# A hybrid decoder block on one core: the output projection in two seven-product parts with tokens on the result's partitions, and last products whose banks begin with a partial sum

## Chip, core and metric

One core of a Trainium2 chip runs the whole program in one launch. The metric is the device time in microseconds (us) of one execution; the number to be predicted is the median of several runs. Engines are named as in the profile: PE (TensorE), DVE (VectorE), ACT (ScalarE), POOL (GpSimd) and SP (SyncE, which here only issues transfers). PEld is PE's loading of the stationary operand.

## The reference

One layer of a decoder, 512 tokens of width 2048, all in fp32. The part that matters here begins with `mix`, the sum of two gated mixers:

```python
mix = (g_a * y_a + g_b * y_b) @ w_o[l]          # (512 x 2048) @ (2048 x 2048)
x = x + gt_a * mix                              # called x2 below
h = _rmsnorm(x, norm_ffn[l]) * (1.0 + sc_f) + sh_f
gate, up = jnp.split(h @ w_gate_up[l], 2, axis=-1)   # 2048 x 11264
x = x + gt_f * ((jax.nn.silu(gate) * up) @ w_down[l])  # 5632 x 2048
return _rmsnorm(x, final_norm)
```

`gt_a`, `sc_f`, `sh_f` and `gt_f` are one value for each of the 2048 channels.

## The kernel before

**Precision.** Every large product is computed from operands split in two: a high half rounded to fp32r (`hi`, made by ACT) and the rest (`lo`, made by DVE). A product is three matmuls, hi·hi, hi·lo and lo·hi, added up in a PSUM bank. Raw weights come from HBM through SP's queue into five `raws` buffers; four `his` and four `los` buffers hold the halves; 68 `slots` of 128 x 512 hold nearly everything else. There are eight PSUM banks of 128 x 512.

**Order.** The work is a list of `Unit`s (load, split, matmuls, `pre`, `post`), which a `Driver` runs with loads and splits some units ahead. Side work stands in generators that are stepped between matmuls. Every operation is recorded (so all have the line number 482 in the profile) and a planner, `Score`, then puts out the instructions: those of PE, POOL and SP stay in the order of the program, those of DVE and ACT are placed by due times from a model of costs.

**The output projection.** Up to this point the activations have channels on the partitions. `yb_done` makes, from four row blocks of `mix` at a time, the operands of a seven-product scheme of matrix multiplication (2 x 2 blocks, seven products instead of eight): a11, a12, a21, a22 and the combinations x5, x6, x7, x3. It also stores a21 in HBM. `strassen_wo(n)` for n = 0, 1, 2 then computes 512 output channels each: eight units, one for each pair of row blocks of 128; in each, the seven products times two halves of 128 channels times three matmuls. The weights are the stationary operand and 256 tokens are the moving one, so results have channels on the partitions. The last 512 channels come from `half_sets`, a plain product for each half of the tokens (h = 0, 1), for which `wo_rest` brings a21 back.

**x2 and its norm.** The results are multiplied by `gt_mix` and added to x (from the transposed input `xT`): for n = 0, 1 by accumulating transfers of POOL's queue into `x2_dram`, which had been filled with a copy of x, and for n = 2 and the plain set in SBUF. `squares` adds up squares over channel tiles; `part_rstd` sums them over partitions with matmuls by a column of ones (`hss`), takes the root on DVE, and `spread` brings it to all partitions with another matmul (`hbc`). For h = 0 this runs under the plain set's second half, for h = 1 under the first gate-up set. `h2_gen(h)` then makes for each pair of channel tiles the scaled and shifted `h2f` and its two halves, `h2T`.

**Gate-up.** `gu0` (h = 0, then h = 1) and `gu_both(1)` are plain products with 256-column matmuls: unit i of 16 reads h2T tile i of its half. From then on `big` uses the seven-product scheme in two parts: `FIRST4` (m1, m6, m7, m5: eight units of 24 matmuls of 512 columns) and `LAST3` (m2, m4, m3: eight units of 18), with tokens on the result's partitions and weight combinations that the first part stores in `s_dram` for the second. `tokens_down` does the same for the down projection.

**The last products.** `last_dn` ends the kernel. Its first 16 units are the last `tokens_down`; meanwhile partial sums come back (`s_t`, from `down_dram`), are multiplied by the row of `gt_f` (`gated`), and x2 is loaded back. Then four row blocks of w_down remain for each token tile t and 512 columns n. `last_weights` multiplies those weights by the row of `gt_f` and splits them. Each `token_unit` begins its bank with four transposes of x2 (`turned`), since x2 has channels on the partitions, and adds the products; `finished` adds s_t to the bank, squares it (with the sum along the row on ACT), multiplies by `final_norm`, and after the last columns of a token tile takes the root and stores. The last tile's columns are done in two halves of 256.

Of the kernel before, what the change touches and what calls it, by code (L numbers as in the profile page):

```python
# [9 lines left out]
F32 = mybir.dt.float32  # L10
# [481 lines left out]
def block_kernel(ctx: ExitStack, tc: tile.TileContext, a: dict, out):  # L492
# [1102 lines left out]
    a21 = [None] * 4  # L1595
    a21_dram = dram.tile([4, P, 512], F32, name="a21_dram")

    def yb_done(n):
        def done(ps):
# [6 lines left out]
            def gen():  # L1606
                a1 = S("a1h", F32R), S("a1l", F32R)
                for i in (2 * n, 2 * n + 1):
# [7 lines left out]
                    side(a21_dram[n, :, c], a21_)  # L1616
                    u, v = S("x56"), S("x73")
                    x5, x6, x7, x3 = (w[:, 256 * h:256 * h + 256] for w in (u, v) for h in range(2))
                    for o, x, y, op in ((x5, a22, a21_, ALU.subtract), (x6, a11, x5, ALU.add), (x7, a11, a21_, ALU.subtract),
                                        (x3, x6, a12, ALU.subtract)):  # L1620
                        nc.vector.tensor_tensor(o, x, y, op)
# [27 lines left out]
    def wo_half(k, h, xi):  # L1649

        n, j = divmod(k, 4)
        i = 2 * n + j % 2
        if j > 1:
            return wo_part("m4" if h else "m2", i, xi)
        return a21[n][xi][:, 256 * (i % 2):256 * (i % 2) + 256] if h else wo_part("m1", i, xi)

    def strassen_wo(n):

        w = a["w_o"][0].rearrange("(n h k p) c -> n k p h c", n=4, h=2, p=P)

        def outputs(res):
            for h in range(2):
                for f in range(2):
                    t, q, gate = res.pop("gp"[f] + str(h)), 2 * n + f, (gt_mneg if f else gt_mix)
                    if n == 2:
                        for k in (2 * q, 2 * q + 1):
                            d = half_of(x2[h][q], k)
                            nc.vector.scalar_tensor_tensor(d, half_of(t, k), gate[:, k:k + 1], d, op0=ALU.mult, op1=ALU.add)
                        squares(q, HALF[h], nc.vector)
                        nc.scalar.dma_start(x2_dram[h, q], x2[h][q][:])  # L1670
                    else:
                        for k in (2 * q, 2 * q + 1):
                            nc.scalar.activation(half_of(t, k), half_of(t, k), AF.Copy, scale=gate[:, k:k + 1])
                        side(x2_dram[h, q], t[:], accum_op=ALU.add)
                    del t
                    yield

        def freed(i):
            if n == 2:
                wo_x["x56"][i] = wo_x["x73"][i] = None  # L1680
                if i == 5:
                    for q in (4, 5):
                        for h in range(2):
                            load_x2(h, q)

        return strassen(lambda i: w[i // 2, i % 2], 512 * n + 256, 512 * n,
                        [(c, i, j, lambda k, c=c: [wo_part(c, k, xi) for xi in range(2)]) for c, i, j in PRODUCTS],
                        wo_ready, outputs, freed)

    def wo_rest():  # L1690

        def x2_back(h):
            for q in range(4):
                x2[h][q] = S("x2")
                side(x2[h][q][:], x2_dram[h, q])

        for h in range(2):
            x2_back(h)
        for n in range(4):
            a21[n] = S("a21")  # L1700
            load(a21[n][:], a21_dram[n])
            yield
        for q in range(4):
            squares(q, HALF[0], nc.vector)
            if q % 2:
                yield
        for n in range(4):
            a21[n] = hilo(a21[n][:], "a21")
            yield
        for q in range(4):  # L1710
            squares(q, HALF[1], nc.vector)
            yield

# [17 lines left out]
    x2 = [[None] * 8 for _ in range(2)]  # L1731
    s_ffn, sh_ffn, gt_mix, gt_ffn, gt_mneg = (C(n, [P, 16]) for n in ("s_ffn", "sh_ffn", "gt_mix", "gt_ffn", "gt_mneg"))
    g_dram = dram.tile([D], F32, name="g_dram")
    x2_dram = dram.tile([2, 8, P, 512], F32, name="x2_dram")
# [6 lines left out]
    def x_part(h, q):  # L1741
        return a["xT"][256 * q:256 * q + 256, 256 * h:256 * h + 256].rearrange("(k p) n -> p k n", p=P)

    def load_x2(h, q):
        x2[h][q] = S("x2")
        load(x2[h][q][:].rearrange("p (k n) -> p k n", k=2), x_part(h, q))

    def copy_x(h, q):
        side(x2_dram[h, q].rearrange("p (k n) -> p k n", k=2), x_part(h, q))

    sums = {}

    def add_gated(h, k, ps, gate, c0=0):

        d = half_of(x2[h][k // 2], k)[:, c0:c0 + ps.shape[1]]
        nc.vector.scalar_tensor_tensor(d, ps, gate[:, k:k + 1], d, op0=ALU.mult, op1=ALU.add)

    def view(tile_, seg):

        return tile_[:].rearrange("p (k n) -> p k n", k=2)[:, :, seg[1]:seg[1] + seg[2]]  # L1760

    def squares(q, seg, eng):

        s = S("sq")
        st = sums.setdefault(seg, [])
        nc.scalar.activation(view(s, seg), view(x2[seg[0]][q], seg), AF.Square)
        if st and eng is not None:
            eng.tensor_tensor(view(st[0], seg), view(st[0], seg), view(s, seg), ALU.add)
        else:
            st.append(s)  # L1770
# [1282 lines left out]
```

## Time and profile before

| | |
|---|---|
| median of 3 runs | 2698.59 us (2698.04 to 2701.13) |
| the profiled execution, its own time | 2699.31 us |
| its span, first to last instruction | 2697.5 us |
| mean granted clock of PE | 0.999 |
| PE busy | 2683.8 us of the span (99%) |
| DVE busy | 2124.2 us (79%) |
| ACT busy | 1168.9 us (43%) |
| transfers | 587.16 MB, mean 218 GB/s |

A matmul's row has a start and a duration that includes its drain, so matmuls that follow each other closely overlap in the rows: 512 columns show 0.39 us each while they start 0.2267 us apart. Paces are therefore taken from stretches of many matmuls, or from starts. A row of the chain of waits reads: start, length, engine and tile, and the number of instructions merged in it. Names of tiles have their final numbers cut off: `x2` appears as `x`, `h2f` stays, `rs` are the small tiles of a root, `dnt` the banks of the last products.

### The profile page before, as it was taken

The numbers are of one execution on the slowest core, as the hardware profiler recorded it, in microseconds if no ns is written. First come the engines' busy times: TensorE is split into PE (matmuls) and PEld (weight loads), VectorE is DVE, ScalarE is ACT, GpSimd is POOL, SyncE is SP. The second block draws the span as 40 slices with busy tenths as digits, with TensorE's granted clock in tenths as the row PEclk, the third lists the DMA queues.
The fourth block names the chain that finished last, engine by engine and source line by source line (L and its number), as shares of the span: only waits on it lengthen the run. The fifth ranks groups of instructions, "written<-read, shape, count | busy, mean of one in ns | idle before, by whom it ended". The sixth has DMA issues, their size and how long they took to land.

```text
span 2697.5 us, 38122 instructions
## 1 busy us (share of the span) xinstructions
PE 2683.8 (99%) x13886; PEld 2277.0 (84%) x13886; DVE 2124.2 (79%) x3259; ACT 1168.9 (43%) x1620; POOL 196.7 (7%) x315
## 2 busy tenths in 40 slices
PE   9999999999999999999999999999999999999998
PEld 7888788888888888889999888888888888888887
DVE  8985656777887887688897777887777888878888
ACT  4343432452245343234574444444444445444434
POOL 0000002001101000000100000000000101010000
PEclk9999999999999999999999999999999999999999
DMA  9995555646566889624864565656556667695694
GB/s 351 348 369 193 165 168 170 199 132 189 166 195 208 302 280 333 235 83 124 258 194 144 189 204 201 211 198 209 188 201 206 212 231 270 198 278 205 222 311 164
DMA packets 308228, 587.16 MB, mean 218 GB/s; under 512 B 42228, under 2 KB 81412, under 8 KB 308040
## 3 DMA queue, kind: packets, MB, share of 16 engines
q1 hardware_dynamic: 267832, 493.60, 55.2%
q0 software_dynamic: 20992, 64.27, 7.3%
q10 hardware_dynamic: 19216, 26.87, 2.8%
q8 instruction: 108, 1.77, 0.3%
q14 instruction: 80, 0.66, 0.1%
HBM read 501.77 MB, written 83.89 MB: 217 GB/s over the span
## 4 chain that ended last, share of the span: by engine, by line
PE 98%; DMA 1%; DVE 0%; ACT 0%; issue 0%; DVEq 0%; SPq 0%
PE m L482 45%; PE gb L482 7%; PE v L482 4%; PE gu L482 3%; PE z L482 3%; PE ya L482 3%; PE ga L482 3%; PE k L482 3%; PE q L482 3%; PE yb L482 3%; PE s L482 3%; PE dnt L482 2%; PE wo L482 2%; PE qk L482 2%; PE cq L482 2%; PE dn L482 2%
## 5 line engine op out<-in xcount | busy, mean ns | idle before, releaser
L482 ACT CAST hi<-raws 128x1024 fp32r<-128x1024 f32 (+2 forms) x360 | 325.8, 905 | 509.7 <-PE m L482 298.8
L482 DVE TENSOR_TENSOR lo<-raws,hi 128x1024 fp32r<-128x1024 f32 (+2 forms) x360 | 369.1, 1039 | 171.1 <-ACT hi L482 167.5
L482 ACT CAST hi<-raw 128x1024 fp32r<-128x1024 f32 (+2 forms) x259 | 268.8, 1038 | 483.0 <-DMA raw<-in_w_in_dram 80.3
L482 DVE TENSOR_TENSOR lo<-raw,hi 128x1024 fp32r<-128x1024 f32 (+2 forms) x259 | 313.3, 1211 | 170.7 <-ACT hi L482 163.0
L482 DVE CUSTOM_DVE_ANT_0 rawm<-rawm,cbc 128x1024 f32<-128x1024 f32 x192 | 232.4, 1224 | 21.7 <-DMA rawm<-in_w_mod_dram 21.4
L482 ACT CAST hi<-sums 128x1024 fp32r<-128x1024 f32 x136 | 143.0, 1051 | 160.3 <-PE m L482 133.7
L482 DVE TENSOR_TENSOR lo<-sums,hi 128x1024 fp32r<-128x1024 f32 x136 | 166.2, 1222 | 47.5 <-ACT hi L482 47.2
L482 PE MATMUL m<-hi,h2h 128*128 128x512 f32 x480 | 189.9, 396 | 0.0
L482 PE MATMUL m<-hi,h2l 128*128 128x512 f32 x480 | 187.2, 390 | 0.0
L482 PE MATMUL m<-lo,h2h 128*128 128x512 f32 x480 | 187.1, 390 | 0.0
L482 PE MATMUL m<-lo,xh 128*128 128x512 f32 x448 | 174.5, 390 | 0.8 <-DVE lo L482 0.8
L482 PE MATMUL m<-hi,xh 128*128 128x512 f32 x448 | 174.4, 389 | 0.0
L482 PE MATMUL m<-hi,xl 128*128 128x512 f32 x448 | 174.3, 389 | 0.0
L482 DVE TENSOR_TENSOR sums<-raws,raws 128x1024 f32<-128x1024 f32 x112 | 136.6, 1219 | 8.8 <-DMA raws<-in_w_down_dram 4.5
L482 POOL DMA_DIRECT2D s_dram<-raws x112 | 60.9, 543 | 679.2 <-DVE raws L482 657.2
L482 PEld LDWEIGHTS m<-hi,h2l 128*128 128x128 f32 x480 | 90.1, 188 | 18.8
L482 PEld LDWEIGHTS m<-lo,h2h 128*128 128x128 f32 x480 | 90.3, 188 | 17.8
L482 PEld LDWEIGHTS m<-hi,h2h 128*128 128x128 f32 x480 | 90.2, 188 | 17.6
L482 PE MATMUL gb<-hh,hi 128*128 128x512 f32 x256 | 101.9, 398 | 0.0
L482 PEld LDWEIGHTS m<-lo,xh 128*128 128x128 f32 x448 | 84.1, 188 | 19.0 <-DVE lo L482 1.7
L482 PE MATMUL gb<-hl,hi 128*128 128x512 f32 x256 | 100.0, 390 | 0.0
L482 PE MATMUL gb<-hh,lo 128*128 128x512 f32 x256 | 99.9, 390 | 0.0
(543 smaller groups left out, 7089.8 us busy)
## 6 DMA issues: line engine op xcount, KB each, us to landing
raws<-in_w_gate_up_dram SPq DMA_DIRECT2D x400, 256.0 KB, 3.6
rawm<-in_w_mod_dram SPq DMA_DIRECT2D x192, 512.0 KB, 5.5
raw<-in_w_in_dram SPq DMA_DIRECT2D x143, 512.0 KB, 4.8
raws<-in_w_down_dram SPq DMA_DIRECT2D x160, 256.0 KB, 4.6
s_dram<-raws POOLq DMA_DIRECT2D x112, 256.0 KB, 3.2
raws<-s_dram SPq DMA_DIRECT2D x112, 256.0 KB, 2.9
rawa<-in_w_in_dram SPq DMA_DIRECT2D x32, 512.0 KB, 3.7
raws<-in_w_o_dram SPq DMA_DIRECT2D x48, 256.0 KB, 3.0
```

The source lines that it names most:

```text
L482: self.tc.keep_in_program_order(op.call(*op.args, **op.kwargs))
```

## The change

Four things change.

1. `tokens_wo(n)` for n = 0, 1 takes the place of the three channel-wise sets and the plain one. It has the form of `big`: activations are the stationary operand, 512 weight columns the moving one, 1024 output channels a part, all with tokens on the result's partitions. The signs of x5, x6 and x3 change for it; a21 is no longer stored. In the second part (n = 1) the product m4 is taken out of the last eight units and done at the very end (`fourth`, eight units of six matmuls), so that tokens 0 to 255 are complete before it starts.
2. x2 is kept by tokens: x comes from an untransposed input, the gate is a row spread over the partitions (`mix_row`), the squares are summed along the row by ACT, and `rooted` takes a root per token on DVE and scales x2 with it. No matmuls by ones remain.
3. `h2_gen` now transposes the scaled x2 on PE, four 128 x 128 tiles to a bank (`hT`), and scales and shifts them out of PSUM: on ACT for h = 0, on DVE for h = 1. It is stepped only by `ahead`, in front of each unit of `gu0`.
4. In the last products no transposes are left. `seeded` writes the bank before its first matmul: for n = 1, 3 DVE writes s_t + x2, for n = 0, 2 (`RAW`) ACT writes s_t. In the RAW columns neither the weights nor s_t are multiplied by the row of `gt_f`; `finished` multiplies the bank instead and adds x2. In the other columns `finished` reads the bank directly for the square and for the product with `final_norm`.

The core of the diff:

```diff
-    def strassen_wo(n):
...
-    def wo_rest():
...
+    def tokens_wo(n):
+        c0, c1 = 1024 * n, 1024 * n + 512
...
+        FIRST4 = [("m1", 0, 1, "m1"), ("m6", 0, 0, "m6"), ("m7", 1, 0, "m7"), ("m5", 1, 1, "m5")]
+        LAST3 = [("m2", 1, 0, "m1"), ("m3", 0, 1, "m5")] if n else [("m2", 1, 0, "m1"), ("m4", 0, 0, "m7"), ("m3", 0, 1, "m5")]
...
+        def start(i):
+            second, k = divmod(i, 8)
+            r = box["r"] = raws.tile([P, 2, 512], F32, tag="raw", name=nm("raws"))
+            b = box["b"] = S("raws")
...                                  # three loads of 128 x 512 each
+        def ready_x(t, f, z):
+            add(x2[t, f][:], x2[t, f][:], z)
+            squared(t, f)
+            side(x2_dram[t][:, 512 * f:512 * f + 512], x2[t, f][:])
+
+        def early():
+            for t in range(2):
+                add(up1[t], up1[t], g_mix[3][:], ALU.mult)
+                ready_x(2 + t, 3, up1[t])
+            for t in range(2):
+                z = S("z")
+                add(z[:], v[t], g_mix[3][:], ALU.mult)
+                add(x2[t, 3][:], x2[t, 3][:], z[:], ALU.subtract)
...
+                            mm(ps[bank][t][:], wo_part(c, k, xi)[:, P * t:P * t + P], box["w"][w][wi][:, j, :],
+                               start=not second and k == 0 and m == 0, stop=k == 7 and m == 2, skip_group_check=True)
...
+        return [unit(i) for i in range(16)] + ([fourth(k) for k in range(8)] if n else [])
+
+    def rooted(h):
+        for t in (2 * h, 2 * h + 1):
+            nc.vector.tensor_reduce(sx[:, t, 4:5], sx[:, t, 0:4], AX.X, ALU.add)
+        ys = [token_root(sx[:, t, 4:5], 1.0 / D) for t in (2 * h, 2 * h + 1)]
+        for n in range(4):
+            for j in range(2):
+                x = S("xn")
+                nc.scalar.activation(x[:], x2.pop((2 * h + j, n))[:], AF.Copy, scale=ys[j][:])
+                x2_out[2 * h + j, n] = x
...
     def h2_gen(h):
-        yield 3 if h else 1
-        diag = part_rstd([HALF[h]])
-        yield 6 if h else 4
-        r = spread(*diag)
         for q in range(8):
-            f = S("h2f")
-            for k in (2 * q, 2 * q + 1):
-                nc.vector.scalar_tensor_tensor(half_of(f, k), half_of(x2[h][q], k), s_ffn[:, k:k + 1], r, op0=ALU.mult, op1=ALU.mult)
-                nc.scalar.activation(half_of(f, k), half_of(f, k), AF.Identity, bias=sh_ffn[:, k:k + 1])
+            ps, f = PS("hT"), S("h2f")
+            for k in (2 * q, 2 * q + 1):
+                for j in range(2):
+                    nc.tensor.transpose(half_of(ps, k)[:, tok(j)], x2_out[2 * h + j, k // 4][:, tok(k % 4)], ident)
...
+            for k in (2 * q, 2 * q + 1):
+                if h:
+                    nc.vector.tensor_scalar(half_of(f, k), half_of(ps, k), s_ffn[:, k:k + 1], sh_ffn[:, k:k + 1], op0=ALU.mult, op1=ALU.add)
+                else:
+                    nc.scalar.activation(half_of(f, k), half_of(ps, k), AF.Identity, scale=s_ffn[:, k:k + 1], bias=sh_ffn[:, k:k + 1])
             h2T[h][q] = hilo(f[:], "h2")
...
-                    def ahead(h=h, k=min(2 * i + 4, KT)):
-                        while h2n[h] < k:
+                    def ahead(h=h, k=2 * i + 4):
+                        while h2n[h] < min(k, KT):
                             drv.step(h2c[h])
+                        while h == 0 and h2n[1] < k - KT:
+                            drv.step(h2c[1])
...
+        wl, x2t, ends, RAW = {}, {}, [], (0, 2)
...
-        def turned(t, n, ps, cs):
...
+        def seeded(t, n, cs):
+            ps, w = PS("dnt"), cs.stop - cs.start
+            if n in RAW:
+                nc.scalar.copy(ps[:, 0:w], s_t[t, n][:, cs])
+            else:
+                nc.vector.tensor_tensor(ps[:, 0:w], s_t[t, n][:, cs], x2t[t, n][:, cs], ALU.add)
+            return ps
 
         def finished(t, n, ps, cs=slice(0, 512)):
...
-            nc.vector.tensor_tensor(xt, xt, ps[:, 0:w], ALU.add)
-            nc.scalar.activation(tmp[:, 0:w], xt, AF.Square, accum_out=sf[:, t, c:c + 1])
+            if n in RAW:
+                tmp = S("sq")
+                nc.vector.tensor_tensor(xt, ps[:, 0:w], rows[n][:, cs], ALU.mult)
+                nc.vector.tensor_tensor(xt, xt, x2t[t, n][:, cs], ALU.add)
+                nc.scalar.activation(tmp[:, 0:w], xt, AF.Square, accum_out=sf[:, t, c:c + 1])
+            else:
+                nc.scalar.activation(xt, ps[:, 0:w], AF.Square, accum_out=sf[:, t, c:c + 1])
+            if not last:
+                nc.vector.tensor_tensor(xt, ps[:, 0:w], rows[4 + n][:, cs], ALU.mult)
...
-                nc.vector.tensor_tensor(raw[:], raw[:], rows[n][:].unsqueeze(1).broadcast_to([P, 2, 512]), ALU.mult)
+                if n not in RAW:
+                    nc.vector.tensor_tensor(raw[:], raw[:], rows[n][:].unsqueeze(1).broadcast_to([P, 2, 512]), ALU.mult)
...
-                    gated(0)
...
-                            if k0 == 2:
+                            if k0 == 2 and 2 + n not in RAW:
                                 u = begin(lambda n=n: gated(2 + n))(u)
```

The x tiles of `tokens_wo` are loaded at fixed units (a table `X_AT`): two in the first part's units 12 and 14, fourteen in the second part's units 0 to 7, as the operands x5, x6 and a1 of the finished products give their slots back. The tiles of x2 in the last products come back by tokens at the places where the transposed ones did.

More of the change, by code (lines that the diff above doesn't have):

```diff
@@ L2822, in finished @@
                     else:
[L2823 removed]
+                        for p_, n_, c_ in ends:
+                            if n_ == i:
+                                nc.vector.scalar_tensor_tensor(o[:, c_], p_[:, 0:c_.stop - c_.start], y[:, 0:1], rows[4 + i][:, c_], op0=ALU.mult, op1=ALU.mult)
                     (nc.scalar.dma_start if i % 2 else load)(out[tok(t), 512 * i:512 * i + 512], o)
```

485 lines of the change are left out of this document (221 added, 264 removed).

## Prediction

> **What bounds the kernel now.** I read the page first, then the waits of TensorE, then the chain of waits that ended last, around the stage that changes and at the end, then busy times by stretch.
>
> ```profile
> PE 2683.8 (99%) x13886; PEld 2277.0 (84%) x13886; DVE 2124.2 (79%) x3259; ACT 1168.9 (43%) x1620; POOL 196.7 (7%) x315
> ```
> ```profile
> PE m L482 <- DVE lo L482: 0.8, 2, 0.5
> ```
> ```profile
> 1201.34 120.95 PE m L482 x1008
> 1322.30 27.36 PE wo L482 x228
> ...
> 1369.68 7.20 PE gu L482 x60
> ...
> 1386.84 76.31 PE gu L482 x636
> ```
> ```profile
> 1463.15 127.87 PE m L482 x564
> ```
>
> TensorE works in 2683.8 of 2697.5 us, and outside the first 18 us and the tail its waits sum to 0.8 us. So a matmul removed is time removed, unless a new wait takes it. The chain gives the paces: 120.95/1008 = 0.120 us for 256 columns, 127.87/564 = 0.2267 us for 512. The output projection takes 1201.34 to 1369.68 (168.3 us), the first two gate-up sets 1369.68 to 1463.15 (93.5 us), neither with a wait.
>
> **Matmuls.** Before: three seven-product sets of 8 x 7 x 2 x 3 = 336 and a plain set of 384, 1392 of 256 columns. After: two parts of 8 x (24 + 18) = 336, 672 of 512 columns: 672 x 0.2267 = 152.3 us. The 768 gate-up matmuls stay at 0.120: 92.2 us. The small matmuls of the norm (sums over partitions, the spread of the scale) go.
>
> ```profile
> L482 PE MATMUL dnt<-kc,x 128*128 128x128 f32 x64 | 9.7, 272 | 0.0
> ```
> ```profile
> 2636.77 0.60 PE L482 MATMUL dnt<-kc,x 128*128 128x128 f32 x4
> 2637.13 0.48 PE L482 MATMUL dnt<-hi,ah 128*128 128x512 f32 x1
> 2637.44 0.39 PE L482 MATMUL dnt<-lo,ah 128*128 128x512 f32 x1
> ```
>
> The 64 transposes of x2 move from the last products to the entry of gate-up. Four of them and one matmul take 2637.44 - 2636.77 = 0.67 us, so four take 0.44 and 64 take 7.0: out at the end, in at gate-up. TensorE work from 1201.34 to the end of gate-up: 152.3 + 92.2 + 7.0 = 251.5 instead of 261.8, minus 10.3; with the 7.0 at the end, **minus 17.3**.
>
> **The entry of gate-up.** In the old order the norm of the first token half ran under the second half's matmuls. In the new one the transposes of the first tile stand directly ahead of the matmuls that need their result: `ahead` issues q = 0 and 1 in front of unit 0, and TensorE goes in order.
>
> ```profile
> 1389.72 0.91 ACT L482 ACTIVATE h2f<-h2f,sh_ffn 128x256 f32<-128x256 f32 x2 [0.20 <-DVE h2f L482]
> 1390.66 0.62 ACT L482 CAST h2h<-h2f 128x512 fp32r<-128x512 f32 x1
> 1391.19 1.05 ACT L482 CAST hi<-raw 128x1024 fp32r<-128x1024 f32 x1
> 1391.32 0.69 DVE L482 TENSOR_TENSOR h2l<-h2f,h2h 128x512 fp32r<-128x512 f32 x1
> ```
>
> Two scalings, the cast and the low half take 1389.72 to 2.29 us later. The second tile's transposes cover 0.44 of it; with hand-offs between engines (0.04 each between these rows) TensorE idles **2.0 us**. Every gate-up matmul queues behind it. A hidden gap is excluded, since TensorE's order is the program's; the lower end is 1.5, the upper end 4, if a weight cast stands ahead of the tile on ScalarE and a weights' low half on VectorE.
>
> Before that, the root chain of tokens 0 to 255 must end under the eight units of the fourth product (48 matmuls, 10.9 us).
>
> ```profile
> 2687.86 0.28 PE L482 MATMUL dnt<-hi,al 128*128 128x256 f32 x1
> 2688.18 0.42 DVE L482 TENSOR_TENSOR sd<-sd,dnt 128x256 f32<-128x256 f32 x1
> 2688.70 0.40 ACT L482 ACTIVATE sq<-sd 128x256 f32<-128x256 f32 x1
> 2689.00 0.18 ACT L482 ACTIVATION_READ_ACCUMULATOR sq<-sd 128x1 f32 x1
> 2689.22 0.16 DVE L482 TENSOR_REDUCE sf<-sf 128x1 f32<-128x5 f32 x1 [0.62 <-ACT sq L482]
> 2691.13 1.42 DVE L482 SCALAR_TENSOR_TENSOR sd<-sd,rs,row 128x512 f32<-128x512 f32 x2
> ```
> ```profile
> 1378.94 0.15 DVE L482 TENSOR_SCALAR rs<-hss 128x2 f32<-128x2 f32 x1
> 1384.36 0.48 DVE L482 TENSOR_SCALAR diag<-kc,rs 128x128 f32<-128x128 f32 x2
> ```
> ```profile
> L482 ACT ACTIVATE sd<-sd,rs 128x512 f32<-128x512 f32 x14 | 9.4, 711 | 1.7 <-DVE rs L482 1.3 <-ACT sd L482 0.4
> ```
>
> The same chain at the kernel's end, on a free VectorE, takes 2688.18 to 2691.13, 2.95 us. Here it has 512 columns, one more multiply and two tiles (about 6 us), then two scalings at 0.71: 7.4, under 10.9. But on a full VectorE a root took 1378.94 to 1384.36, 5.4 us instead of 1.9; 3.5 more would end at the limit. I charge **1.0**, ends 0 and 4. Within gate-up ScalarE must give per unit a weight cast (1.05), two scalings (0.91), a cast (0.62) and one scaling by the root (0.71), about 3.2 us with their overlaps, against 24 x 0.120 + 0.44 = 3.3: **1.0**, ends 0 and 4.
>
> **VectorE and the queues in the second part.**
>
> ```profile
> 1384.76 1.22 DVE L482 TENSOR_TENSOR lo<-raw,hi 128x1024 fp32r<-128x1024 f32 x1
> 1385.89 0.69 DVE L482 TENSOR_TENSOR h2l<-h2f,h2h 128x512 fp32r<-128x512 f32 x1
> 1386.49 0.87 DVE L482 SCALAR_TENSOR_TENSOR h2f<-x,s_ffn,hbc 128x256 f32<-128x256 f32 x2
> ```
> ```profile
> 1282.00:1322.00 40.00, 40.00 (x335) 40.00 (x335) 30.14 (x41) 21.62 (x29) 6.92 (x11) 1.00 0.83 243
> 1370.00:1393.00 23.00, 23.00 (x193) 22.95 (x192) 22.38 (x47) 18.98 (x30) 0.00 (x0) 1.00 0.54 166
> 2620.00:2637.00 17.00, 16.48 (x75) 13.29 (x74) 15.73 (x21) 6.35 (x7) 0.00 (x0) 1.00 1.01 368
> 2637.00:2661.00 24.00, 24.00 (x123) 19.93 (x122) 23.42 (x29) 8.90 (x16) 0.00 (x0) 1.00 0.48 176
> 2661.00:2685.00 24.00, 24.00 (x122) 19.87 (x121) 19.16 (x48) 12.03 (x27) 0.00 (x0) 1.00 0.22 83
> ```
>
> Starts 1.13 and 0.60 us apart are the paces of 1024 and 512 elements. A four-product unit needs 3 x 1.13 + 0.60 = 4.0 us of VectorE for 24 x 0.2267 = 5.4 of TensorE, a later unit 2.3 for 4.1, in the second part 2.3 for 2.7. The second part adds the first part's outputs (eight tiles, multiply and add: 9.6, and 2.4 of sums), 3.6 of sums, 4.8 in `early`, 4.8 for the next four tiles, about 3 of roots and 2.3 of gate-up splits: 32 + 18.6 + 30.5 = 81 us against 76.2 of TensorE. Two units (8.0) are split on entry, so 73 of 76, 96%. The row 1370 to 1393 (columns: length, busy PE, PEld, DVE, ACT, POOL, clock, DMA share, GB/s) shows 22.38 of 23.00 with TensorE at 23.00: that can be carried. One place is closer than the mean: there m3 follows m2 after 6 matmuls (1.36 us), and VectorE must have read m5 out of the same banks by then. **1.0** for the part, ends 0 and 5.
>
> The queues: SP gets 16 loads of x and 4 of rows among its weight loads, where it had 8 of x and 4 of a21. POOL loses 16 copies, 8 accumulations, 8 loads of x2 and 8 stores of a21, and gets 16 stores of sums, 16 of x2 and one row. ACT loses 8 stores of x2. Per four-product unit of the second part that is three weight tiles, one store of sums, about two x tiles and one store of x2, 7 x 262 KB in 5.44 us or 337 GB/s. The traces carried 368 at a share of 1.01, so it fits at 92% while loads are issued two units ahead. I charge nothing; the cover gone is a rival below.
>
> **The last products.** TensorE takes 51.4 us (2636.77 to 2688.14) and would take 44.4. VectorE is busy 42.6 us up to 2685 and some 2 more up to the last matmul. Inside the stage one gate of four tiles (2.4) and two multiplies of weights (2.3) go, and the eight results of columns 0 and 2 need one more operation each (4.8); as much again goes ahead of it, where loads hold the stage. So about 45 us of VectorE stand against 44 of TensorE: **1.1**, ends -0.8 (the two waits for `lo` go) and 4. The seeds themselves (0.60 each) lie beside other products, since banks come free a product ahead. In the tail the 256-column add (2688.18 to 2688.70) leaves the chain and one short operation enters: **minus 0.3**.
>
> Sum: -17.3 + 2.0 + 1.0 + 1.0 + 1.0 + 1.1 - 0.3 = -11.5. The profiled execution took 2699.31, 0.7 over the median of the runs: 2687.8 for it, **2687** for the median.
>
> **Rivals.**
>
> *The gap trips the clock.*
>
> ```profile
> 2690.00:2692.00 2.00, 0.00 (x0) 0.00 (x0) 1.79 (x8) 0.87 (x2) 0.00 (x0) 0.59 0.84 311
> 2692.00:2694.00 2.00, 0.00 (x0) 0.00 (x0) 0.55 (x1) 0.47 (x1) 0.00 (x0) 0.50 0.66 246
> ```
> ```profile
> 4.99 6.21 PE L482 MATMUL warm<-wide,ones_r 128*128 128x512 f32 x14
> 11.04 0.40 PE L482 MATMUL s<-hh,hi 128*128 128x512 f32 x1
> ```
>
> After the last matmul (2688.14) the granted clock went to half: 0.59 over 2690 to 2692 means 0.36 us at full, so at 2690.4, 2.2 us of idleness. At the start fourteen warm-up matmuls took 0.44 each, double pace, and full pace held from 11.04. A gap of 3 us or more at gate-up's entry would then run up to 8 us at half pace, 4 us lost, and 2 more in the gap: 2693. For it: my gap lies just under 2.2. Against: one tile's chain is short and transposes resume inside it. The Trainium skill's page "TensorE: Matmul & The Clock Gate" (section "HAM oscillation — how this bites in real kernels") says that idle gaps over about 3.4 us return TensorE to half rate; by its window 1.7 us would be lost. The trace's drop after 2.2 us is earlier than that figure. Chance 0.14.
>
> *VectorE becomes the bound* at the second part and in the last products: if the two units split ahead are not there on entry, 5 us come back, and 4 in the last products: 2694 to 2696. For it: 96% and 102% above. Against: 22.38 of 23 carried. Chance 0.14.
>
> *SP's queue starves the weights; slower.*
>
> ```profile
> raw<-in_w_o_dram SPq DMA_DIRECT2D x16, 512.0 KB, 6.7
> ```
>
> In the second part the x loads wait in SP's queue for buffers that the preceding unit's products free, and weight loads wait behind them. With no lead a unit takes 6.7 of landing, about 1 of cast and 1.13 of low half, 8.9 instead of 5.4: 8 units lose 28 us, 2715. It decides from 1.5 us lost per unit, that is, when the lead falls below 7.4 us; the code issues loads at least two units (10.9 us) ahead. Against: 92% of the transfer rate is not more than it. Chance 0.08.
>
> *It nets to nothing*, by upper ends of several terms: within 5.4 us of 2698.6. Chance 0.04.
>
> **How the numbers follow.** The forecast (2682 to 2691) has 0.60. The measurement tells 0.2%, 5.4 us, from no change: faster means under 2693.2. The clock case falls on that bound (0.11 faster, 0.03 same), the VectorE case on both sides of it (0.07 and 0.07), the last two are 0.08 slower and 0.04 same. Faster 0.60 + 0.11 + 0.07 = 0.78, same 0.03 + 0.07 + 0.04 = 0.14, slower 0.08. The low end is -17.3 with a gap of 1.5, the tail and the two waits for `lo` gone, -16.9, or 2682; the high end takes in the clock case and most of the VectorE case, 2695.
>
> **What would show it.** Right: 672 matmuls of `m` at 0.2267 with no 256-column ones between `yb` and `gu`; one wait of TensorE of about 2 us at the first `gu` matmul, released by the low half of `h2`, clock 1.00 after it; the last products near 44 us. Wrong: TensorE waits for `lo` or for DMA inside the second part, ScalarE's `h2` rows releasing every gate-up unit, or seeds releasing `dnt` matmuls.

## The result and the profile after

| | before | after |
|---|---|---|
| median of the runs | 2698.59 us (2698.04 to 2701.13, 5 runs) | 2688.51 us (2685.82 to 2690.38, 5 runs) |
| the profiled execution, its own time | 2699.31 us | 2687.51 us |
| its span | 2697.5 us | 2685.7 us |

The changed kernel is faster by 10.1 us: its time is 0.996 of the time before, 95% interval 0.9946 to 0.9975. The forecast was 2687, with a range from 2682 to 2695. The total came out; several of its terms did not.

First the page's line of busy times, then the waits of TensorE in the changed kernel (engine and tile, what released it, us in total, times, longest), without the waits of the kernel's first 18 us.

```profile
PE 2667.5 (99%) x13146; PEld 2235.0 (83%) x13146; DVE 2118.3 (79%) x3224; ACT 1171.2 (44%) x1629; POOL 194.2 (7%) x316
```
```profile
PE gu L482 <- ACT h2h L482: 1.7, 1, 1.7
PE m L482 <- DVE w4l L482: 1.3, 1, 1.3
PE gu L482 <- DVE h2l L482: 0.3, 1, 0.3
```

TensorE has 740 instructions and 16.3 us of busy time less. The two waits for `lo` (0.8) are gone. Three new waits took their place, 3.3 us together, and all lie at two spots: the last product of the second part, and the entry of gate-up.

The timeline around that entry and the chain of waits behind it show the gap and what followed.

```profile
1355.24 1.10 PE L482 MATMUL hT<-kc,xn 128*128 128x128 f32 x8
1358.02 0.38 PE L482 MATMUL gu<-h2h,hi 128*128 128x256 f32 x1 [1.69 <-ACT h2h L482]
1358.74 0.38 PE L482 MATMUL gu<-h2l,hi 128*128 128x256 f32 x1 [0.34 <-DVE h2l L482]
```
```profile
1358.74 4.50 PE gu L482 x23
1363.70 2.87 PE gu L482 x24
...
1458.90 11.13 PE m L482 x49
```
```profile
1358.00:1360.00 2.00, 1.64 (x10) 1.44 (x11) 2.00 (x3) 1.97 (x4) 0.00 (x0) 0.94 0.91 301
1360.00:1362.00 2.00, 2.00 (x12) 2.00 (x11) 1.90 (x3) 1.10 (x2) 0.00 (x0) 0.50 0.59 155
1362.00:1364.00 2.00, 2.00 (x14) 2.00 (x14) 0.36 (x1) 0.93 (x1) 0.00 (x0) 0.71 0.64 183
```

The gap is 1.69 + 0.34 = 2.03 us. Then the column that gives the clock falls to 0.50. The missing shares, 0.06 + 0.50 + 0.29 of 2 us each, mean 2 x 1.7 = 3.4 us at half pace. The 23 matmuls behind the gap took 4.50 us; the later 24 took 2.87. So about 1.7 us went there. Gate-up ends at 1458.90, where it had ended at 1463.15.

The stretch of the second part, where the new loads lie, and the first and last matmul of the last products:

```profile
1280.00:1323.00 43.00, 43.00 (x191) 35.54 (x191) 40.51 (x48) 22.34 (x33) 6.48 (x12) 1.00 0.90 308
```
```profile
2631.38 0.39 PE L482 MATMUL dnt<-hi,ah 128*128 128x512 f32 x1
...
2674.93 0.28 PE L482 MATMUL dnt<-hi,al 128*128 128x256 f32 x1
```

TensorE is busy all 43 us at 308 GB/s and a DMA share of 0.90, with VectorE at 40.51. The last products run from 2631.38 to 2675.21, 43.8 us instead of 51.4, and wait for nothing. But the tail behind the last matmul is 2685.7 - 2675.21 = 10.5 us; it was 2697.5 - 2688.14 = 9.4. VectorE's rows of the tail say why.

```profile
2675.80 0.16 DVE L482 TENSOR_REDUCE sf<-sf 128x1 f32<-128x5 f32 x1
...
2676.37 0.22 DVE L482 SCALAR_TENSOR_TENSOR rs<-rs,rs 128x1 f32<-128x1 f32 x1
2676.51 0.69 DVE L482 TENSOR_TENSOR sd<-dnt,row 128x512 f32<-128x512 f32 x1
2677.11 0.60 DVE L482 SCALAR_TENSOR_TENSOR rs<-rs,rs 128x1 f32<-128x1 f32 x3
2677.62 0.69 DVE L482 TENSOR_TENSOR sd<-sd,row 128x512 f32<-128x512 f32 x1
2678.22 0.41 DVE L482 SCALAR_TENSOR_TENSOR rs<-rs,rs 128x1 f32<-128x1 f32 x2
```

Two multiplies left over from the tile before (0.69 each) stand between the short steps of the last root. The root takes 2675.80 to 2678.63, 2.8 us; before, on a free VectorE, 2689.22 to 2691.1, 1.9. VectorE's load in the last products did not stop TensorE: it was carried as a backlog into the tail.

The account, by the starts of first matmuls: the output projection begins at 1201.16 instead of 1201.18; from there to the end of gate-up it is 257.6 us instead of 261.8, -4.2; the middle is 1172.6 instead of 1173.8, -1.1; the last products -7.5; the tail +1.1. Before rounding that makes -11.8, the difference of the spans.

### The profile page after: what moved, and what is told of

Same layout as the page of the kernel before. It is cut to its first block, busy times and chain, and to the rows that moved or that the text cites. A ratio compares the mean times of both kernels' runs of the same rounds, so it can differ in the third digit from the quotient of the medians.

```text
span 2685.7 us, 36647 instructions
## 1 busy us (share of the span) xinstructions
PE 2667.5 (99%) x13146; PEld 2235.0 (83%) x13146; DVE 2118.3 (79%) x3224; ACT 1171.2 (44%) x1629; POOL 194.2 (7%) x316
## 3 DMA queue, kind: packets, MB, share of 16 engines
q8 instruction: 103, 1.69, 0.3%
## 4 chain that ended last, share of the span: by engine, by line
PE 93%; issue 3%; DMA 1%; DVE 1%; ACT 1%; POOL 0%; SPq 0%; ACTq 0%; POOLq 0%; DVEq 0%
PE m L482 41%; PE gb L482 7%; PE v L482 4%; PE gu L482 4%; PE z L482 3%; PE ya L482 3%; PE k L482 3%; PE ga L482 3%; PE q L482 3%; PE yb L482 3%; PE s L482 3%; PE qk L482 2%; PE cq L482 2%; PE dn L482 2%; PE ckv L482 2%
## 5 line engine op out<-in xcount | busy, mean ns | idle before, releaser
L482 ACT CAST hi<-raws 128x512 fp32r<-128x512 f32 (+1 forms) x376 | 344.2, 916 | 552.0 <-PE m L482 302.5
L482 DVE TENSOR_TENSOR lo<-raws,hi 128x512 fp32r<-128x512 f32 (+1 forms) x376 | 390.1, 1053 | 173.2 <-ACT hi L482 169.4
L482 ACT CAST hi<-raw 128x1024 fp32r<-128x1024 f32 (+1 forms) x243 | 251.9, 1037 | 466.0 <-DMA raw<-in_w_in_dram 64.0
L482 DVE TENSOR_TENSOR lo<-raw,hi 128x1024 fp32r<-128x1024 f32 (+1 forms) x243 | 293.8, 1210 | 152.7 <-ACT hi L482 149.4
L482 PE MATMUL m<-hi,xh 128*128 128x512 f32 x576 | 224.1, 389 | 0.0
L482 PE MATMUL m<-lo,xh 128*128 128x512 f32 x576 | 224.1, 389 | 0.0
L482 PE MATMUL m<-hi,xl 128*128 128x512 f32 x576 | 224.1, 389 | 0.0
L482 DVE TENSOR_TENSOR sums<-raws,raws 128x1024 f32<-128x1024 f32 x128 | 156.2, 1220 | 17.9 <-DMA raws<-in_w_down_dram 9.8
L482 PEld LDWEIGHTS m<-hi,xl 128*128 128x128 f32 x576 | 108.1, 188 | 22.5
L482 PEld LDWEIGHTS m<-lo,xh 128*128 128x128 f32 x576 | 108.1, 188 | 22.5
L482 PEld LDWEIGHTS m<-hi,xh 128*128 128x128 f32 x576 | 108.1, 188 | 22.4
```

What stands on the lines that cost most here:

```text
L482: self.tc.keep_in_program_order(op.call(*op.args, **op.kwargs))
```

## The experiments

Each kernel is the changed one with the edit shown. Two groups of four ran on two chips, each with its own runs of the kernel before (medians 2699.55 and 2700.23), so the ratio to these is given; the changed kernel's was 0.996 (0.9946 to 0.9975). The interval of each experiment's ratio overlaps with this one. The planner orders VectorE and ScalarE anew for each kernel, and places that an edit doesn't touch then move by 1 or 2 us; four executions of the one changed kernel have spans from 2685.2 to 2688.4. So every verdict rests on the stretch of the trace that the edit is about.

**Fill the gap.**

```diff
+                if h == 0:
+                    junk = lambda: mm(st["ps"][3][:, 0:128], ones_r[:], ones_r[:], start=True, stop=True)
+                    half[0].mms = [junk] * 26 + half[0].mms
```

> The changed kernel with 26 extra matmuls of 128 columns (ones by ones, about 1.75 us in all) put on TensorE between the first transposes of x2 and the first gate-up matmul; their result is overwritten. Theory (idleness of about 2 us at that place lets the granted clock fall to half for some 3.4 us): the wait of 1.69 us turns into busy time, the clock stays at 1.00 between 1358 and 1364 us, the first gate-up unit takes 2.9 us instead of 4.5, the median falls by about 1.5 us to 2687. Rival (the dip has another cause, such as the transposes or the transfers that run then): the clock still reads about 0.5 there and the time stays at 2688.5.

Measured: 2686.14 us (2684.43 to 2687.59), ratio 0.9948 (0.9934 to 0.9961). The wait of TensorE, where it lies, the extra matmuls, and the windows behind the entry:

```profile
PE m L482 <- DVE euvw L482: 1.8, 1, 1.8
```
```profile
1324.67 0.50 PE L482 MATMUL m<-hi,xh 128*128 128x512 f32 x1 [1.77 <-DVE euvw L482]
```
```profile
1357.12 3.10 PE L482 MATMUL gu<-ones_r 128*128 128x128 f32 x26
```
```profile
1358.00:1360.00 2.00, 2.00 (x20) 2.00 (x20) 1.80 (x3) 1.97 (x5) 0.00 (x0) 1.00 0.97 296
1360.00:1362.00 2.00, 1.86 (x15) 1.66 (x15) 1.25 (x3) 2.00 (x5) 0.00 (x0) 1.00 0.84 254
```

With matmuls in the gap the clock stays at 1.00 there. One profile alone would not show that the idleness cost the half pace, since one kernel below kept its clock with the gap open. All profiles together do: of nine executions with a gap of 1.9 us or more at this place eight fell to half pace, and of the three kernels without it (this one and the two with the early tile below) none. But not every wait of that length does it: in this kernel TensorE waits 1.77 us up to 1324.67, among matmuls of 512 columns, and the clock reads 1.00 from 1322 to 1330.

The gap itself remains, filled, and more than filled: the extra matmuls start 0.113 us apart, not the 0.067 that the 1.75 us had assumed, and the first gate-up matmul comes at 1360.05, 3.7 us behind the start of the transposes instead of 2.8. The profiled span did not fall (2685.8 against 2685.7): from the transposes to the end of gate-up 0.9 us were gained, and 1.1 were lost ahead of them, half of it in the wait of 1.8 us that stands in place of the 1.3 for `w4l`. There m3 waits until VectorE has read m5 out of its banks. That is the place that the prediction had named as closer than the mean; in the changed kernel it did not wait.

**The first tile's transposes ahead of the last unit of the output projection.**

```diff
+                if n and i == 23:
+                    def first_tile():
+                        h2c[0] = [h2_gen(0), 0]
+                        drv.step(h2c[0])
+                    with_pre([u], first_tile)
...
-                for h in range(2):
-                    h2c[h] = [h2_gen(h), 0]
+                h2c[1] = [h2_gen(1), 0]
```

> The changed kernel with the first tile's four transposes, scaling and split issued in front of the last of the eight units of the fourth product, not in front of gate-up. Theory (the gap comes from the program order of TensorE alone): the 2.03 us of waiting shrink to 0.5 us or less plus up to 0.5 us of waiting for the scaled x2, the clock does not fall, and the median falls by 2.5 to 3.5 us, to about 2685.5. Rival (the root of tokens 0 to 255 on a full VectorE is what ends last): the wait only moves ahead of the transposes and the clock still falls, 2688.

Measured: 2683.27 us (2682.66 to 2684.05), ratio 0.9939 (0.9926 to 0.9951), the profiled span 2681.3. The waits and the chain behind the entry:

```profile
PE gu L482 <- ACT h2h L482: 0.4, 1, 0.4
PE gu L482 <- DVE h2l L482: 0.3, 1, 0.3
```
```profile
1355.92 3.02 PE gu L482 x23
```

These are all its waits past the start. The 1.4 us of matmuls of the last unit cover most of the tile's chain, and 23 matmuls take 3.02 us instead of 4.50. Of the 4.4 us between the spans, 1.3 is the gap, about 1.5 the clock, and 1.3 a wait for `w4l` that this order happens not to have. This version beats both kernels: its slowest run, 2684.05, is below the changed kernel's fastest, 2685.82 (2686.99 on the same chip, further down). Only the same edit with another order of the last products, below, is level with it.

**The low halves of the fourth product's weights on GpSimd.**

```diff
-                w4[k] = hilo(box["b"][:], "w4")
+                w4[k] = S("w4h", F32R), S("w4l", F32R)
+                nc.scalar.copy(w4[k][0][:], box["b"][:])
+                nc.gpsimd.tensor_tensor(w4[k][1][:], box["b"][:], w4[k][0][:].bitcast(F32), ALU.subtract)
```

> The changed kernel with the low halves of the fourth product's weights (eight operations of 512 elements, about 5 us of VectorE) made on GpSimd. Theory (VectorE is the bound in the second part, 0.6 us of 81 over what is to be had): TensorE's wait of 1.25 us for such a low half goes and the root is ready earlier; the median falls by 1 to 2 us, to about 2687. Rival (the wait is a matter of order and latency, not of VectorE's load): the wait stays on another low half, or GpSimd's slower operation makes it longer; 2688.5 or more.

Measured: 2691.07 us (2689.86 to 2692.68), ratio 0.9968 (0.9955 to 0.998). The wait for `w4l` is gone, yet VectorE is as busy as before. Its groups over 1323 to 1357 us (busy us, mean ns), first in the changed kernel, then in this one, with GpSimd's:

```profile
L482 DVE TENSOR_TENSOR lo<-raws,hi 128x1024 fp32r<-128x1024 f32 x6 | 7.2, 1220 | 2.0 <-ACT hi L482 2.0
L482 DVE TENSOR_TENSOR x<-x,z 128x512 f32<-128x512 f32 x6 | 4.1, 686 | 0.1
L482 DVE TENSOR_TENSOR z<-m,row 128x512 f32<-128x512 f32 x4 | 2.6, 682 | 0.0
```
```profile
L482 DVE TENSOR_TENSOR lo<-raws,hi 128x1024 fp32r<-128x1024 f32 x6 | 9.8, 1652 | 1.4 <-ACT hi L482 1.4
L482 DVE TENSOR_TENSOR x<-x,z 128x512 f32<-128x512 f32 x6 | 6.5, 1104 | 0.1
L482 DVE TENSOR_TENSOR z<-m,row 128x512 f32<-128x512 f32 x4 | 2.6, 676 | 0.0
```
```profile
L482 POOL TENSOR_TENSOR w4l<-raws,w4h 128x512 fp32r<-128x512 f32 x7 | 10.5, 1516 | 4.0 <-ACT w4h L482 2.5 <-issue 1.4
```

Beside GpSimd's subtractions VectorE's operations with two inputs in SBUF grow from 1220 to 1652 ns and from 686 to 1104. These are means, also over operations that no subtraction overlaps; a single 128 x 512 one took 1740 ns (1346.68 to 1348.42, beside GpSimd's row of three subtractions from 1345.04 to 1349.58). The one that reads a matmul's bank stays at 682 and 676, though three of its four lie beside that row. The work taken off VectorE came back as slower work (31.6 and 32.0 us busy of the 34), the wait for `w4l` was replaced by one of 2.1 us for `xn` and one of 0.7 for `lo`, and the gap at the entry grew to 2.7. The Trainium skill's page "GPSIMD Engine Reference" (section "1. Specifications") lists GpSimd's SBUF interfaces as shared with VectorE, with contention where a VectorE instruction has two SBUF inputs. These rows agree.

**Other columns begin with the raw sum** (0 and 1 instead of 0 and 2, so that the last token tile's third block has no multiply and add behind it).

```diff
-        wl, x2t, ends, RAW = {}, {}, [], (0, 2)
+        wl, x2t, ends, RAW = {}, {}, [], (0, 1)
...
-                    gated(1)
```

> The changed kernel with columns 0 and 1 instead of 0 and 2 as those whose weights and partial sums are not multiplied by the gate's row. The longer finish of such columns then lies earlier, and VectorE has 2.4 us more to do inside the last products and 2.4 less ahead of them. Theory (the end after the last matmul grew from 9.4 to 10.5 us because the finish of tile (3, 2) has two operations more): the end shrinks to about 9.2 us and the time falls by about 1 us, to 2687.5. Rival (VectorE's load in the whole stage sets the end): the end stays at 10.5 us or TensorE waits among the last products, the time grows by 1 to 2 us.

Measured: 2689.02 us (2686.41 to 2690.44), ratio 0.9959 (0.9947 to 0.9972). A wait, and VectorE's rows of the last root:

```profile
PE dnt L482 <- DVE dnt L482: 2.0, 1, 2.0
```
```profile
2679.50 0.16 DVE L482 TENSOR_REDUCE sf<-sf 128x1 f32<-128x5 f32 x1 [0.52 <-ACT sd L482]
...
2680.07 1.31 DVE L482 SCALAR_TENSOR_TENSOR rs<-rs,rs 128x1 f32<-128x1 f32 x6
2681.30 0.69 DVE L482 TENSOR_TENSOR sd<-sd,row 128x512 f32<-128x512 f32 x1
```

The root is whole again, 2679.50 to 2681.30, and the tail is 9.2 us, as the theory had it. But now a seed that VectorE writes comes 2.0 us late, as the rival had it. Matmuls and tail together take 55.3 us instead of 54.3, where this choice of columns, by the count above, puts 2.4 us more of VectorE's work into the stage. In these two orders VectorE's load shows either in the tail or in a seed.

**Half the lead of the weight loads.**

```diff
-                drv.ahead = 2
+                drv.ahead = 1
```

> Weight loads of the output projection and of the first gate-up set are issued one unit ahead instead of two; the arithmetic is the changed kernel's. In the changed kernel the second part (1280 to 1323 us) ran with no wait of TensorE at 308 GB/s and a DMA share of 0.90. Theory (the lead has slack, and the load queue was never close to starving the weights): no new wait of TensorE for a load, the stage within 1 us, the median 2687 to 2691. Rival (the queue was close to the edge, and it took the second unit of lead to carry the second part): a four-product unit needs 8.9 us from issue to low half against 5.4 of TensorE, so with the lead halved some of the eight units lose 1 to 3.5 us each, TensorE waits for a weights' half at 10 to 25 us in all, and the median is 2699 to 2713.

Measured: 2688.99 us (2687.9 to 2690.89), ratio 0.9958 (0.9945 to 0.9972). The waits in the output projection:

```profile
PE m L482 <- DVE euvw L482: 0.9, 1, 0.9
PE m L482 <- DVE lo L482: 0.8, 1, 0.8
PE m L482 <- DVE w4l L482: 0.3, 1, 0.3
```

2.0 us of waits instead of 1.3, one of them (0.8) for a weights' low half, none for a load; the output projection takes 155.5 us instead of 154.1. The starvation of 10 to 25 us is refuted, even with the lead halved.

**No seeds in the last products.**

```diff
-            if n in RAW:
-                nc.scalar.copy(ps[:, 0:w], s_t[t, n][:, cs])
-            else:
-                nc.vector.tensor_tensor(ps[:, 0:w], s_t[t, n][:, cs], x2t[t, n][:, cs], ALU.add)
+            if n not in RAW:
+                nc.vector.tensor_tensor(s_t[t, n][:, cs], s_t[t, n][:, cs], x2t[t, n][:, cs], ALU.add)
...
+            nc.vector.tensor_tensor(xt, ps[:, 0:w], xt, ALU.add)
+            ps = xt
...
-                        start=False, stop=last, skip_group_check=True))
+                        start=(k, x, y) == (0, 0, 0), stop=last, skip_group_check=True))
```

> In the last products alone the banks no longer begin with the partial sum: the first matmul starts the bank, and the partial sum is added by VectorE afterwards; 17 additions of 512 or 256 columns (0.69 or 0.42 us) come onto VectorE behind the products, about 11 us, and eight copies of 0.60 leave ScalarE. Theory A (the last 7 us gained come from the 64 transposes that left, and VectorE at 42 of 44 us is the limit of this stage, so what is put on it shows): the stage has 44 us of matmuls and 53 of VectorE, TensorE waits or the tail grows by 6 to 10 us together, the median 2695 to 2699. Theory B (the seeds are what takes the stage from 51 to 44 us only by keeping adds out of the tail; in mid-stage VectorE has slack in what lies between): only the tail grows by the additions of its last tiles, 1 to 2 us, the median 2689.5 to 2691.

Measured: 2694.14 us (2690.62 to 2696.43, 11 runs), ratio 0.9976 (0.9967 to 0.9985). Busy times over the last stage, and its first and last matmul:

```profile
2640.00:2650.00 10.00, 10.00 (x46) 8.29 (x45) 10.00 (x14) 3.17 (x3) 0.00 (x0) 1.00 0.45 165
2650.00:2660.00 10.00, 10.00 (x46) 8.28 (x45) 10.00 (x16) 4.68 (x10) 0.00 (x0) 1.00 0.00 0
...
2680.00:2692.00 12.00, 0.00 (x0) 0.00 (x0) 9.85 (x29) 7.25 (x17) 0.00 (x0) 0.53 0.50 184
```
```profile
2634.31 0.39 PE L482 MATMUL dnt<-hi,ah 128*128 128x512 f32 x1
...
2677.86 0.28 PE L482 MATMUL dnt<-hi,al 128*128 128x256 f32 x1
```

The matmuls still take 43.8 us (2634.31 to 2678.14), without a wait, so the 7.5 us of that stage come from the 64 transposes that left, as the forecast had it. VectorE is at 10.00 of 10 in two windows, and the tail is 2694.6 - 2678.14 = 16.5 us, 6.0 more. About 10 us were put on VectorE; what found no room beside the matmuls ended up behind them. The mechanism is theory A's, at the low end of its 6 to 10 us; the median lies between the two theories' figures, a little below A's. The profiled span is 8.9 us above the changed kernel's, and the other 2.9 are not this edit's: they lie ahead of the stage, 1.3 of them in a wait for `euvw` near 2602.

**Another order of the last products.**

```diff
-            for t, n in ((0, 2), (1, 2), (0, 3), (1, 3), (2, 2), (2, 3)):
+            for t, n in ((0, 2), (1, 2), (0, 3), (1, 3), (2, 2), (3, 2), (2, 3)):
                 yield token_unit(t, n)
-            yield token_unit(3, 2, free=True)
```

> The order of the last products is changed: the third column block of the last token tile is computed ahead of the fourth block of the tile before it, so that its longer finish (multiply, add, squares) has 2.7 us more before the last matmul. The tail after the last matmul was 10.5 us in the changed kernel, 9.36 before the change. Theory (the tail's 1.1 us is the two VectorE operations of that block on the chain): the tail returns to about 9.4, the median falls by about 1 to 2687.5. Rival (the tail is VectorE's and ScalarE's whole load, and the order only moves it): the root and the four scalings of the tile before (4 x 0.7 us on ScalarE) now end 2.7 us later and stand in front of the last tile's squares, the tail grows by 1 to 2 us, the median 2689.5 to 2690.5.

> The first tile's transposes ahead of the last output-projection unit, as in the earlier run of that edit (2683.27 against 2699.55 before the change), together with the new order of the last products. If the two are independent, the time is that run's plus what the order alone gives: 2682 by the theory that the tail falls by 1 us, 2684.5 to 2685.5 by the rival that it grows. A wait at gate-up's entry of 0.4 + 0.3 us and the clock at 1.00 there, as in that run; if the clock dips to half there again at so short a gap, the length of the gap is not what trips it.

Measured: 2686.61 us (2685.72 to 2688.01), ratio 0.995 (0.9938 to 0.9963); with the early tile 2683.29 (2682.5 to 2683.36), ratio 0.9937 (0.9924 to 0.9949), what the early tile gives alone. The last matmul ends at 2673.67 of 2684.2: the tail is 10.5 us, as in the changed kernel. Neither theory held. The third block's two operations left the chain, and two multiplies of the tile before stood in the root as they had.

What shortened the span was at the other place. The first gate-up matmul and the window in which the changed kernel ran at half pace, in the new order without the early tile:

```profile
1357.94 0.39 PE L482 MATMUL gu<-h2h,hi 128*128 128x256 f32 x1 [1.68 <-ACT h2h L482]
```
```profile
1360.00:1362.00 2.00, 2.00 (x20) 2.00 (x19) 1.89 (x3) 1.42 (x3) 0.00 (x0) 1.00 0.58 163
```

The same wait, and no fall of the clock: gate-up takes 1.5 us less, which is the whole difference of the spans (2684.2 and 2685.7).

**The same program three times.**

> The changed kernel again, unaltered, for one more profiled execution. In its first profile TensorE waited 1.69 + 0.34 us at gate-up's entry and the granted clock went to half 1.8 us after the first gate-up matmul, for 3.6 us; in the run with the new order of the last products the same two waits stood there and the clock stayed at 1.00. Theory (the length of the wait alone does not decide; the clock is judged over a window whose position differs from execution to execution): among three executions of this one program some dip and some do not, and the spans differ by about 1.6 us, near 2685.7 with the dip and 2684.1 without. Rival (something in this program, such as where its waits lie, decides): all three dip alike, spans within 0.5 us of 2685.7.

> The second of the three executions: by the theory the clock in the 8 us behind gate-up's entry and the span are either those of the first profile (half pace for 3.6 us) or 1.00 throughout with a span about 1.6 us shorter; by the rival always the former.

> The third of the three executions, with the same two expectations: by the theory either half pace for 3.6 us or clock 1.00 and about 1.6 us less; by the rival always half pace.

Measured: times 2687.48, 2690.19 and 2686.99 us, spans 2685.7, 2688.4 and 2685.2. All three have the wait of 1.69 us and all three fall to half pace. For the first and the third, the first gate-up matmul and the windows with a clock below 1.00:

```profile
1358.23 0.43 PE L482 MATMUL gu<-h2h,hi 128*128 128x256 f32 x1 [1.69 <-ACT h2h L482]
```
```profile
1358.00:1360.00 2.00, 1.47 (x6) 1.23 (x7) 1.79 (x3) 1.97 (x5) 0.00 (x0) 0.61 0.88 280
1360.00:1362.00 2.00, 2.00 (x11) 2.00 (x11) 1.89 (x4) 1.32 (x2) 0.00 (x0) 0.54 0.49 133
```
```profile
1356.63 0.39 PE L482 MATMUL gu<-h2h,hi 128*128 128x256 f32 x1 [1.69 <-ACT h2h L482]
```
```profile
1356.00:1358.00 2.00, 1.03 (x6) 0.83 (x7) 1.39 (x2) 1.97 (x4) 0.00 (x0) 0.97 0.82 272
1358.00:1360.00 2.00, 2.00 (x11) 2.00 (x11) 1.89 (x4) 1.72 (x3) 0.00 (x0) 0.50 0.49 149
1360.00:1362.00 2.00, 2.00 (x14) 2.00 (x14) 0.98 (x1) 0.21 (x1) 0.00 (x0) 0.68 0.67 227
```

The missing shares sum to 0.85 in both, (0.39 + 0.46) and (0.03 + 0.50 + 0.32), which is 3.4 us at half pace each time; the second execution and the first profile give the same. What differs is the onset. In the first of the three, 0.61 over 1358 to 1360 puts it at 1358.44, 0.2 us after the first gate-up matmul; in the third, 0.97 over 1356 to 1358 puts it at 1357.88, 1.25 us after; in the first profile 0.94 puts it at 1359.76, 1.7 us after. So the fall starts at a moment that the gap does not fix, and lasts 3.4 us. That none of the three was spared is what the rival said; that the onset moves is what the theory said.

The record of the clock in the traces tells more. Within each trace all changes between full and half pace lie on one grid of 3.413 us. A fall lasts one period; in the GpSimd run, where 2.1 us of waiting stand ahead of the transposes too, it lasted two, 6.8 us. From the return to full pace to the fall in the tail it is 1314.1 us in the first profile and 1317.5 in the three executions here: 385 and 386 periods. So one can work out how the waits at the entry lie on the grid. In the eight executions that fell, the period that ended where the fall began held 1.6 to 2.3 us of waiting. In the new order, counted back from the fall in its tail, a boundary lies at 1357.12, inside the wait, and the two periods held 0.86 and 1.16 us. That fits a clock that is decided period by period, and it would be why this kernel was spared; it was not tested by moving the gap.

Waiting alone is not the measure. The wait of 1.77 us in the first experiment lies inside one period, and so do 1.59 us of the wait for a seed in the raw-column run; both stand among matmuls of 512 columns, and no fall followed. In the second execution a fall at 805.2 follows a period without any wait, filled mostly with 32 matmuls of 64 x 64 and eight of one column. In the first profile the period begins at 1356.33, where the transposes end, so the transposes are not needed for the fall. What counts besides waiting stays open.

The Trainium skill's page "TensorE: Matmul & The Clock Gate" (section "Part 1: The HAM clock gate (the "warmup" mystery)") describes an activity window of about 3.4 us that runs freely and does not restart when a kernel does. The length of 3.4 us and the moving onset agree with it. Its rule that gaps have to exceed about 3.4 us does not agree: 2.0 us of waiting were enough here in four executions of this kernel out of four.

The second execution's span is 2.7 us longer than the first's mostly for another reason: its clock fell once more, from 805.2 to 808.6 us, in a stage that the change does not touch, which cost 1.7; its wait for `w4l` is 0.5 longer. So such falls can be part of the scatter of this kernel's runs.

## Why the prediction was right, and where not

**Matmuls, -17.3.** Right. The output projection took 1201.16 to 1355.24, 154.1 us, where the forecast's 152.3 and the measured wait of 1.3 make 153.6. The last products lost 7.5 us, where 7.0 was forecast for the transposes; the run without seeds has the same 43.8 us, so it is the transposes that left and not the seeds that shortened them.

**The gap, 2.0.** Measured 2.03, at the forecast place. The prediction had one wait, released by the low half; it was two, 1.69 released by ScalarE's cast and 0.34 by the low half.

**"Clock 1.00 after it".** Wrong. This is the step that failed. The prediction set its gap just under the 2.2 us that the tail of before showed, and took that as safe. The tail had shown one onset in one execution; in the tails of the other kernels here the fall comes 2.1 to 5.0 us behind the last matmul, and at the entry it comes 0.2 to 1.7 us behind the end of the wait for the cast. So the 2.2 us was no length of idleness that the clock allows. As a rival the fall was priced at 4 us of lost pace and a gap of 3 us or more; it came at a gap of 2.03 and cost 1.7, the figure that the prediction had worked out from the page's window.

**Root chain, 1.0, and ScalarE in gate-up, 1.0.** Both too high. `xn` did not hold up the transposes, and no wait for ScalarE stands behind the entry. From the first transpose to the first matmul after gate-up it is 1355.24 to 1458.74, 103.5 us; without the gap (2.0) and the clock (1.7) that is 99.8 against 99.2 of matmuls and transposes, and the 0.6 lies in no named wait.

**VectorE in the second part, 1.0.** Measured 1.3, but at the fourth product, not at the place that the prediction had called closest. That place showed itself in two other orders (1.8 and 0.9 us for `euvw`), so it is as close as was said. Where the wait falls differs with the order of VectorE's queue. Moving these subtractions to GpSimd did not buy it off.

**The last products, 1.1, and the tail, -0.3.** The mechanism was right, VectorE as the limit, and the term was put in the wrong place. TensorE never waited; the backlog went behind the last matmul, where the forecast had a gain of 0.3 and 1.1 were lost. Together 0.8 was forecast, and with 43.8 us of matmuls instead of 44.4, 0.5 came. The raw-column run moved it from the tail to a seed, and about 10 us more of VectorE added 6.0 to the tail.

**The load queue, nothing.** Right: 308 GB/s without a wait, and no wait for a load with half the lead.

The sum of -11.5 against -11.8 is thus partly luck. It lacked the clock's 1.7, the tail's 1.4, 0.3 of the wait for `w4l`, 0.6 in gate-up and 0.5 in the output projection, 4.5 in all. Against that stood 2.0 of charges for the root chain and ScalarE that did not come, 1.7 at the last products (a charge of 1.1 and 43.8 instead of 44.4), and 1.1 in the middle, most of it the two waits for `lo` that had been counted only in a lower end, 4.8 in all.

## What to carry to other kernels

A short step that stands directly in front of its own consumer on an in-order engine costs its whole chain of hand-offs; issue it one unit earlier, as the early tile did for 1.3 us of waiting and about 1.5 of pace. Where a gap of some 2 us on TensorE remains, count with a half-pace stretch behind it (1.7 us here, in eight of nine executions at this place), even if a drop seen elsewhere came later than the gap is long. Where VectorE is nearly full beside the matmuls, look for its excess behind the last matmul and not only in waits, and don't expect to shed it to GpSimd while VectorE's own operands lie in SBUF.

## What the runs showed of the hardware

- After waits of 1.69 and 0.30 to 0.34 us at the entry of gate-up the granted clock was at half for 3.4 us in each of four executions, beginning 0.2 to 1.7 us after the first wait's end; in one kernel with the same waits it did not fall, nor with 0.4 + 0.3 us of waiting, nor after a wait of 1.77 us among matmuls of 512 columns.
- The clock's changes lay on a grid of 3.413 us within each trace; the period ahead of each fall at the entry held 1.6 to 2.3 us of waiting, and where a boundary split the waits into 0.86 and 1.16 no fall came.
- An elementwise subtraction on GpSimd (1516 ns for 128 x 512) lengthened VectorE's operations with two SBUF inputs around it by 35% to 61% in the mean (1220 to 1652, 686 to 1104 ns), and left one that reads a matmul's bank at 676.
